# Attention scores ordered behind the mixing products, attention shifted to a later stage, and the state-space scan done in one instruction

## The chip, the cores and the metric

One core of one Trainium2 chip runs the whole layer. The metric is the device time of one execution in microseconds (us). The core has a matrix engine (PE, TensorE), three engines for elementwise work (DVE, which is VectorE; ACT, which is ScalarE; POOL, which is GpSimd) and a queue that issues the DMAs (SP). Each engine works through its own list of instructions in order; semaphores between the lists hold an instruction back until its operands are there.

## The reference

A hybrid block over a sequence of 2048 tokens with 1024 channels, in float32. Two token mixers work side by side on one projection of the normalised input; their outputs are normalised, concatenated and projected back, and a squared-ReLU MLP with 4096 hidden units follows.

```python
xn = rmsnorm(h, norm1_g)
q, k, v, u = split(xn @ w_in)                      # 4 x 512 channels
z = q @ k.T / 8                                    # 8 heads of 64, strictly causal
log_one_minus = where(mask, -softplus(z), 0)
tail = reversed_cumsum(log_one_minus) - log_one_minus
a = where(mask, exp(log_sigmoid(z) + tail), 0)     # stick-breaking weights
sb = a @ v
states = associative_scan(lam_bar, bu)             # 32 groups of 64 complex states
y = gelu(real(states @ c) + d * u)
ssm = y * sigmoid(y @ w_glu + b_glu)
h = h + concat(rmsnorm(sb), rmsnorm(ssm)) @ w_out
out = h + square(relu(rmsnorm(h) @ W1)) @ W2
```

## The kernel before

The sequence is reversed on the host, so that causal sums run forward, and is cut into four quarters of 512 tokens. Matrix operands of the large products are split into a high and a low part, and `mm3` makes each product of three matmuls (high by high, high by low, low by high). Because of that split every product needs an ACT instruction (the high part) and a DVE instruction (the low part) for each operand.

The work is written as Python generators, "streams". `run` takes the next piece from the stream whose virtual time is least; a piece adds its own estimate divided by the stream's weight. So a weight below 1 makes a stream come more seldom. The text order that comes of it is only a priority: a scheduler below it lays out the final list of each engine, with a model of times of its own, and puts an instruction that is ready early ahead of one that is ready late. The lists are then fixed. The stages are:

- `proj_stream` beside `ssm_stream`: 64 jobs of 24 products (1536 matmuls named `m<-w,x`) make q, k, v and u. In the SSM, 16 chains (4 channel blocks, 2 halves of groups, 2 halves of the sequence) each transpose u, multiply by `BT`, rotate by a table (`EC`, `E2`), scan four groups, rotate back into one tile `X`, and multiply by `CP` and `M` (matmuls `m<-CP,X` and `m<-M,uT`); `outputs` then applies GELU. `tables` makes the tables of each block.
- `proj_stream` beside `attn_stream`, in weights 1.0 and 1.0, until the projection is done. A unit of attention is 128 queries of a head against 512 keys; there are 320 units. A unit has two score matmuls (`z`), two ACT sigmoids, a DVE scan (`C`), a POOL multiply, four transposes (`at`), an ACT and a DVE split (`hi`, `lo`) and two matmuls with v (`o`). The transposes and the value products of a unit come seven units behind its scores. A quarter g has 4 - g key blocks for each head, of which one is diagonal and smaller.
- `mix_stream` for the quarter that needs the least (tokens 1536 on) beside attention, weights 1.0 and 1.0. `mix_front` (the gate, 48 products), `mix_body` (the output projection, 192 products) and `mix_tail` (the norm) use products named `m<-h,w 128x512`, 240 in all.
- `plain_up` (1536 products, first MLP layer of two quarters), `mix_stream` for the other quarters in blocks of 256 tokens (`m<-h,w 128x256`, 1440 products), and attention with weight 0.75, until attention has ended.
- `fast_down` for the first half of the output beside the last two blocks of mixing, then `fast_up` and `fast_down` for the other half (products `g`, `fx`, `fy`, `fz`).

Each stage takes its buffers from what the one before it gave back. In the trace the first score starts at 398.6 us, the last projection matmul at 543.5, the first mixing product at 596.3, and the last value product of attention at 1541.4.

Of the kernel before, what the change touches and what calls it, by code (L numbers as in the profile page):

```python
# [62 lines left out]
TWO_PI_INV = 0.6366197723675814  # L63


class Kern:
    def __init__(self, tc, A, out, S):
        self.tc, self.nc, self.A, self.out, self.S = tc, tc.nc, A, out, S
        self.flags = set()
        self.unit = 0  # L70
        self.blocked = {}
# [20 lines left out]
    def mm3(self, ps, lh, ll, rh, rl, start, stop, onto=False):  # L92
        mm = self.nc.tensor.matmul
        mm(ps, lh, rh, start=start, stop=False, skip_group_check=onto)  # L94
        mm(ps, lh, rl, start=False, stop=False, skip_group_check=onto)  # L95
        mm(ps, ll, rh, start=False, stop=stop, skip_group_check=onto)  # L96
# [10 lines left out]
    def consts(self, pool):  # L107
        nc, A = self.nc, self.A
        self.sm = pool.tile([128, NSMALL], F32, name="sm")
        nc.sync.dma_start(out=self.sm, in_=A["small"])  # L110
        self.ident = pool.tile([128, 128], F32, name="ident")
        self.J = pool.tile([128, 128], F32, name="J")
        self.mz = pool.tile([128, 641], F32, name="mz")
        self.ones = pool.tile([128, 128], F32, name="ones")
# [11 lines left out]
    def proj_pools(self, es):  # L126
        tp = lambda n, b: self.pool(es, n, b)
        self.p_xraw = tp("xraw", 2)
        self.p_x = tp("xhl", 4)
        self.p_wraw = tp("wraw", 4)  # L130
        self.p_w = tp("whl", 9)
        self.p_p = tp("pp", 5)
# [128 lines left out]
    def evac(self, Q, gi, j, ps, st, i):  # L261
# [13 lines left out]
        else:  # L275
# [26 lines left out]
            self.pend.append((i + 4, fin))  # L302
# [22 lines left out]
    def attn_stream(self):  # L325
# [30 lines left out]
        def emit_z(b, u):  # L356
            g, h, c = b
            i0 = 128 * u if c == g else 0
            z = self.ps_z.tile([128, 512], F32, tag="z", name="z")
            for m in range(2):  # L360
                nc.tensor.matmul(z[:, i0:512], qt[g, h][m][:, u * 128:(u + 1) * 128], kt[b][:, i0:512],  # L361
                                 start=(m == 0), stop=(m == 1))
            zt[b, u] = z
# [159 lines left out]
    def ssm_params(self):  # L523
# [6 lines left out]
        t = [mk(f"pt{i}") for i in range(6)]  # L530
        ti = mk("pti", W, I32)
        dt = mk("dt")
# [3 lines left out]
        x = mk("px")  # L536
# [5 lines left out]
        sn, cs = mk("sn"), mk("cs")  # L542
        self.sincos(eng, sn, cs, x, t)
        yield 10.0
        lr, li = mk("lr"), mk("li")
# [28 lines left out]
        w1, w2 = mk("pw1", [128, 32, 4]), mk("pw2", [128, 32, 4])  # L574
# [18 lines left out]
        t = [mk(f"pu{i}") for i in range(2)]  # L593
# [26 lines left out]
    def ssm_pools(self, es):  # L620
# [4 lines left out]
        self.m_t = tp("mt", 4)  # L625
        self.m_w = tp("mw", 2)

    def ssm_stream(self):
# [62 lines left out]
        def tables(st, q):  # L691
# [5 lines left out]
            CP = mk("CP", [128, 4, 9, 16])  # L697
            M = Ms[q]
            sl = slice(4 * q, 4 * q + 4)
            gq = slice(8 * st + 4 * q, 8 * st + 4 * q + 4)  # L700
            tabs[st, q] = (EC, E2, BT, CP, M)
# [27 lines left out]
            tt(dve, CP, CP, c1, ALU.add)  # L729
            yield 3.0  # L730
# [12 lines left out]
        def chain(st, q, half):  # L743
# [8 lines left out]
            u2 = self.m_w.tile([128, 4, 8, 16], F32, tag="u2", name="u2", bufs=1)  # L752
# [7 lines left out]
            EC, E2, BT, CP, M = tabs[st, q]  # L760
            X = self.m_w.tile([128, 4, 129], F32, tag="X", name="X", bufs=3)
            Xr = X[:, :, 1:129]
# [13 lines left out]
            for i in range(4):  # L776
                nc.vector.tensor_tensor_scan(
                    out=Xr[:, i, :], data0=prm["rho8"][:, g0 + i:g0 + i + 1].to_broadcast([128, 128]),
                    data1=Xr[:, i, :], initial=0.0 if half else cy[:, i, 3:4], op0=ALU.mult, op1=ALU.add)
            t1, t2 = T([128, 4, 128]), T([128, 4, 128])  # L780
            tt(pool, t1, Xr, EC, ALU.mult)
            nc.scalar.activation(out=t2[0:64], in_=Xr[64:128], func=ACTF.Copy)
            nc.scalar.activation(out=t2[64:128], in_=Xr[0:64], func=ACTF.Copy)
            tt(dve, t2, t2, E2, ALU.mult)
            tt(pool, Xr, t1, t2, ALU.add)
            if half == 1:
                nc.vector.memset(X[:, :, 0:1], 0.0)
                nc.vector.tensor_copy(out=cy[:, :, 0:1], in_=X[:, :, 128:129])
# [5 lines left out]
                tt(dve, cy[:, :, 3:4], cy[:, :, 1:2], cy[:, :, 2:3], ALU.subtract)  # L794
            else:
                nc.vector.tensor_copy(out=X[:, :, 0:1], in_=cy[:, :, 0:1])
# [4 lines left out]
            for i in range(4):  # L801
                o = ps[:, i * 128:(i + 1) * 128]
                nc.tensor.matmul(o, X[:, i, 0:128], CP[:, i, 0:8, :].rearrange("p j h -> p (j h)"),
                                 start=True, stop=False)
                nc.tensor.matmul(o, uT[:, i, :], M[:, i, :], start=False, stop=True)
# [5 lines left out]
        def outputs(st, half):  # L811
            yT = self.m_w.tile([128, 128, 8], F32, tag="c", name="yT", bufs=5)
            for q in range(2):
                ps = self.ps_s.tile([128, 512], F32, tag="m", name="m")
                for i in range(4):
                    nc.tensor.transpose(ps[:, i * 128:(i + 1) * 128], ytm[st, half][:, 4 * q + i, :], self.J)
                a, b = T([128, 512]), T([128, 512])
                nc.scalar.activation(out=a, in_=ps, func=ACTF.Square)
                ts(pool, a, a, 0.044715, ALU.mult, 1.0, ALU.add)
                tt(dve, a, a, ps, ALU.mult)  # L820
                nc.scalar.activation(out=b, in_=a, func=ACTF.Sigmoid, scale=1.5957691216057308)
                tt(dve, yT[:, :, 4 * q:4 * q + 4].rearrange("p c t -> p t c"),
                   b.rearrange("p (t c) -> p t c", t=4), ps.rearrange("p (t c) -> p t c", t=4), ALU.mult)
# [140 lines left out]
    def mix_front(self, X, t0):  # L964
# [12 lines left out]
        for o in range(4):  # L977
            wn = self.load_wt(X, "w_glu", o + 1, 0, 4) if o < 3 else None
            ps = X.ps.tile([128, 512], F32, tag="m", name="m")
            for k in range(4):  # L980
                self.mm3(ps[:, :TB], w[:, 0, k, :], w[:, 1, k, :], yhl[k][:, 0], yhl[k][:, 1], k == 0, k == 3)
                if k % 2:
                    yield mc
# [8 lines left out]
    def mix_body(self, X, b):  # L992
# [6 lines left out]
        for pi, (k0, kk) in enumerate(passes):  # L999
# [5 lines left out]
            for o in range(8):  # L1005
# [9 lines left out]
                for k in range(kk):  # L1015
                    m = b.m[k0 + k]
                    self.mm3(ps[:, :TB], w[:, 0, k, :], w[:, 1, k, :], m[:, 0], m[:, 1], k == 0, k == kk - 1)
# [391 lines left out]
    def run(self, streams, until=None, flag=None):  # L1409
# [3 lines left out]
        while live and flag not in self.flags:  # L1413
# [17 lines left out]
            try:  # L1431
                r = next(gen)
# [9 lines left out]
    def build(self, stop=None):  # L1442
        with ExitStack() as es0:
# [3 lines left out]
            with ExitStack() as el:  # L1447
# [12 lines left out]
                self.run({"proj": (proj, 1.0), "attn": (attn, 1.0)}, until="proj")  # L1460
# [101 lines left out]
```

## Time and profile before

| | |
|---|---|
| median of 3 runs | 2597.24 us (2592.36 to 2602.13) |
| the profiled execution | 2593.43 us, of which the span of the profile is 2591.5 us |
| PE | 2434.2 us busy (94%), 12032 matmuls |
| weight loads (beside PE) | 2009.2 us (78%) |
| DVE | 1943.8 us (75%), 2765 instructions |
| ACT | 1381.3 us (53%), 2628 instructions |
| POOL | 1136.3 us (44%), 1058 instructions |
| HBM | read 395.84 MB, written 134.22 MB |

Matmuls are pipelined: the busy time of one holds its latency, so that a stage can have a nearly full PE row and still issue fewer matmuls in a microsecond than it could. The number of matmuls in a stretch (the x in the tables) is the second thing to read. The product of 128 by 128 by 512 columns is one matmul record; a float32 matmul that isn't of the split kind is recorded as two.

### The profile page before, as it was taken

What the parts mean: (1) busy time and instruction counts of PE and PEld (TensorE: products, weight loads), DVE (VectorE), ACT (ScalarE), POOL (GpSimd) and SP (SyncE); (2) the same over time, 40 slices, a digit from 0 to 9 for tenths busy, and PEclk for the clock granted to TensorE, in tenths of its full rate; (3) what the DMA queues carried; (4) which work ended last, traced back from release to release, by engine and by line L of the source; (5) the groups of instructions that cost most, each with busy time, mean ns of one, the idle gap of its engine ahead of it and who ended that gap; (6) DMA issues with size and microseconds to landing.
All of it is one profiled execution on the core that took longest, in us unless ns stands there. A gap on an engine that the chain in (4) does not pass through costs nothing. (4 is left out here: it accounts for less than half of the span.)

```text
span 2591.5 us, 37361 instructions
## 1 busy us (share of the span) xinstructions
PE 2434.2 (94%) x12032; PEld 2009.2 (78%) x12032; DVE 1943.8 (75%) x2765; ACT 1381.3 (53%) x2628; POOL 1136.3 (44%) x1058
## 2 busy tenths in 40 slices
PE   8898899987888999999999997998999999999999
PEld 6776678865666888888788876886887888887887
DVE  7699978789898787687968863658767666667765
ACT  6454557666465666565656652434444444444443
POOL 5696778678474655464758851140010000003001
PEclk9999999998898999999999998999999999999999
DMA  8635358664563767667786658885674444486565
GB/s 293 201 112 159 118 165 259 174 214 144 175 191 116 252 207 237 223 218 253 254 280 226 216 189 292 298 292 181 207 240 154 142 159 150 145 306 223 180 201 192
DMA packets 352835, 533.74 MB, mean 206 GB/s; under 512 B 34176, under 2 KB 170112, under 8 KB 345344
## 3 DMA queue, kind: packets, MB, share of 16 engines
q1 hardware_dynamic: 352640, 531.36, 62.8%
q8 instruction: 95, 1.56, 0.2%
q14 instruction: 100, 0.82, 0.1%
HBM read 395.84 MB, written 134.22 MB: 205 GB/s over the span
## 5 line engine op out<-in xcount | busy, mean ns | idle before, releaser
L81 POOL TENSOR_TENSOR a<-a,C 128x512 f32<-128x512 f32 (+2 forms) x320 | 437.0, 1372 | 254.9 <-DVE C L385 115.5
L94 PE MATMUL m<-h,w 128*128 128x512 f32 (+1 forms) x1072 | 378.7, 355 | 18.6 <-DMA w<-gluS 9.4
L95 PE MATMUL m<-h,w 128*128 128x512 f32 (+1 forms) x1072 | 376.5, 352 | 5.2 <-DVE h L81 5.2
L96 PE MATMUL m<-h,w 128*128 128x512 f32 (+1 forms) x1072 | 376.4, 352 | 2.5 <-DVE w L81 2.3
L95 PE MATMUL g<-hl 128*128 128x512 f32 x896 | 352.1, 393 | 10.3 <-DVE hl L81 10.3
L96 PE MATMUL g<-hl 128*128 128x512 f32 x896 | 350.8, 392 | 0.0
L385 DVE TENSOR_TENSOR_SCAN C<-s,C,mz 128x513 f32<-128x513 f32 x192 | 305.6, 1600 | 34.9 <-ACT s L376 21.2
L94 PE MATMUL g<-hl 128*128 128x512 f32 x896 | 316.5, 394 | 6.0 <-ACT hl L1138 6.0
L81 POOL TENSOR_TENSOR s<-s,w 128x512 f32<-128x512 f32 x32 | 45.1, 1412 | 486.8 <-DMA ar<-aS 431.7
L1138 ACT ACTIVATE hl<-s 128x512 fp32r<-128x512 f32 x192 | 120.5, 630 | 246.4 <-DVE s L81 92.2
L94 PEld LDWEIGHTS m<-h,w 128*128 128x128 f32 x1072 | 207.3, 194 | 49.6 <-issue 9.9
L95 PEld LDWEIGHTS m<-h,w 128*128 128x128 f32 x1072 | 207.5, 194 | 32.3 <-DVE h L81 6.8
L96 PEld LDWEIGHTS m<-h,w 128*128 128x128 f32 x1072 | 207.1, 193 | 30.0 <-DVE w L81 5.6
L81 DVE TENSOR_TENSOR lo<-at,hi 128x512 fp32r<-128x512 f32 (+1 forms) x320 | 186.4, 593 | 51.6 <-ACT hi L405 51.3
L376 ACT ACTIVATE s<-z 128x512 f32<-128x512 f32 (+1 forms) x320 | 172.9, 541 | 90.1 <-PE z L361 83.4
L405 ACT ACTIVATE hi<-at 128x512 fp32r<-128x512 f32 (+1 forms) x320 | 171.0, 539 | 86.4 <-PE at L401 74.5
L94 PE MATMUL m<-w,x 128*128 128x512 f32 x512 | 207.8, 408 | 8.6 <-ACT w L165 6.0
L95 PE MATMUL m<-w,x 128*128 128x512 f32 x512 | 206.7, 404 | 7.0 <-DVE w L166 7.0
L95 PEld LDWEIGHTS g<-hl 128*128 128x128 f32 x896 | 169.7, 189 | 48.1 <-DVE hl L81 13.4
L96 PE MATMUL m<-w,x 128*128 128x512 f32 x512 | 205.9, 403 | 0.5 <-DVE x L81 0.5
L94 PEld LDWEIGHTS g<-hl 128*128 128x128 f32 x896 | 169.7, 190 | 42.9 <-ACT hl L1138 8.0
L81 DVE TENSOR_TENSOR hl<-s,hl 128x512 fp32r<-128x512 f32 x192 | 137.4, 718 | 83.3 <-ACT hl L1138 78.7
(264 smaller groups left out, 5801.3 us busy)
## 6 DMA issues: line engine op xcount, KB each, us to landing
w<-in_w_dram SPq DMA_DIRECT2D x256, 256.0 KB, 3.6
ar<-aS SPq DMA_DIRECT2D x224, 256.0 KB, 3.4
w<-outS SPq DMA_DIRECT2D x48, 1024.0 KB, 6.4
w<-in_w_dram SPq DMA_DIRECT2D x64, 512.0 KB, 4.2
wr<-in_w_in_dram SPq DMA_DIRECT2D x80, 256.0 KB, 3.8
k<-kS SPq DMA_DIRECT2D x160, 128.0 KB, 3.5
v<-vS SPq DMA_DIRECT2D x80, 256.0 KB, 4.3
aS<-df SPq DMA_DIRECT2D x64, 256.0 KB, 3.0
```

What stands on the lines that cost most here:

```text
L81: eng.tensor_tensor(out=out, in0=a, in1=b, op=op)
L94: mm(ps, lh, rh, start=start, stop=False, skip_group_check=onto)
L95: mm(ps, lh, rl, start=False, stop=False, skip_group_check=onto)
L96: mm(ps, ll, rh, start=False, stop=stop, skip_group_check=onto)
L376: nc.scalar.activation(out=s1[:, 1 + i0:513], in_=z[:, i0:512], func=ACTF.Sigmoid, scale=-0.125)
L385: nc.vector.tensor_tensor_scan(out=C[:, 0:513], data0=s1[:, 0:513], data1=self.mz[:, 128:641], initial=self.C[(n - 4) % 6][:, 512:513], op ...
L405: nc.scalar.activation(out=hi[:, :n], in_=at[:, :n], func=ACTF.Copy)
L1138: nc.scalar.activation(out=t[:, 0], in_=src, func=ACTF.Copy)
```

## The change

Three things are edited together.

The weights of the streams: attention beside the projection goes from 1.0 to 0.55; in the first mixing stage the mixing goes from 1.0 to 2.0; beside the first MLP layer attention goes from 0.75 to 0.95. The `gate`: in the first mixing stage each pair of score matmuls gets an edge that keeps it, in the list of PE alone, behind the last mixing product that was written before it. No semaphore is added.

The SSM chain: the four scans of 128 columns become one scan of 512, whose factor comes from a tile `R` in which the first column of each group is zero; the carried state is added to that column beforehand. The rotation back no longer makes one tile: `Y1` (by `EC`, on POOL) and `Y2` (by `E2`, on DVE) go to PE apart, with a table `CS` that is the swapped and negated `CP`, so each group has three matmuls instead of two. The two DVE multiplies of half height before the scan become two ACT copies and one DVE multiply. GELU drops a POOL instruction, and its transposes now write the tokens interleaved.

Buffers: three weight tiles are read ahead in the projection instead of four (`NW`, `wraw`), `pp` goes from 5 to 4 and the turn of q and k follows three jobs later instead of four; `mt` goes from 4 to 5, and small tables live in shared tiles.

```diff
-        NW = 4
+        NW = 3
...
-            self.pend.append((i + 4, fin))
+            self.pend.append((i + 3, fin))
...
+            with self.tc.issue_after(self.gate) if self.gate else nullcontext():
+                for m in range(2):
+                    nc.tensor.matmul(z[:, i0:512], qt[g, h][m][:, u * 128:(u + 1) * 128], kt[b][:, i0:512],
+                                     start=(m == 0), stop=(m == 1))
...
+            nc.scalar.activation(out=R, in_=prm["rho8"][:, gq].unsqueeze(2).to_broadcast([128, 4, 128]), func=ACTF.Copy)
+            nc.gpsimd.memset(R[:, :, 0:1], 0.0)
...
+            for a, b in ((0, 64), (64, 0)):
+                nc.scalar.activation(out=CS[a:a + 64], in_=CP[b:b + 64, :, 0:8, :].rearrange("p g j h -> p g (j h)"),
+                                     func=ACTF.Copy, scale=-1.0)
...
+            nc.scalar.activation(out=t2[0:64], in_=P[64:128], func=ACTF.Copy)
+            nc.scalar.activation(out=t2[64:128], in_=P[0:64], func=ACTF.Copy)
             tt(dve, t1, P, EC, ALU.mult)
-            tt(dve, t2[0:64], P[64:128], E2[64:128], ALU.mult)
-            tt(dve, t2[64:128], P[0:64], E2[0:64], ALU.mult)
-            tt(pool, Xr, t1, t2, ALU.add)
+            tt(dve, t2, t2, E2, ALU.mult)
+            tt(pool, t1, t1, t2, ALU.subtract)
...
-            for i in range(4):
-                nc.vector.tensor_tensor_scan(
-                    out=Xr[:, i, :], data0=prm["rho8"][:, g0 + i:g0 + i + 1].to_broadcast([128, 128]),
-                    data1=Xr[:, i, :], initial=0.0 if half else cy[:, i, 3:4], op0=ALU.mult, op1=ALU.add)
-            tt(pool, t1, Xr, EC, ALU.mult)
-            nc.scalar.activation(out=t2[0:64], in_=Xr[64:128], func=ACTF.Copy)
-            nc.scalar.activation(out=t2[64:128], in_=Xr[0:64], func=ACTF.Copy)
-            tt(dve, t2, t2, E2, ALU.mult)
-            tt(pool, Xr, t1, t2, ALU.add)
+            nc.vector.tensor_tensor_scan(out=flat(t1), data0=flat(R), data1=flat(t1), initial=0.0,
+                                         op0=ALU.mult, op1=ALU.add)
+            tt(pool, Y1[:, :, 1:129], t1, EC, ALU.mult)
+            tt(dve, Y2[:, :, 1:129], t1, E2, ALU.mult)
...
-                nc.tensor.matmul(o, X[:, i, 0:128], CP[:, i, 0:8, :].rearrange("p j h -> p (j h)"),
+                nc.tensor.matmul(o, Y1[:, i, 0:128], CP[:, i, 0:8, :].rearrange("p j h -> p (j h)"),
                                  start=True, stop=False)
+                nc.tensor.matmul(o, Y2[:, i, 0:128], CS[:, i], start=False, stop=False)
...
-                self.run({"proj": (proj, 1.0), "attn": (attn, 1.0)}, until="proj")
+                self.run({"proj": (proj, 1.0), "attn": (attn, 0.55)}, until="proj")
...
-                self.run({"mix3": (self.mix_stream(X, [1536]), 1.0), "attn": (attn, 1.0)}, until="mix3")
+                self.run({"mix3": (self.mix_stream(X, [1536]), 2.0), "attn": (attn, 1.0)}, until="mix3", gated=True)
...
-                self.run({"attn": (attn, 0.75), "mix": mix, "up": up}, until="attn")
+                self.run({"attn": (attn, 0.95), "mix": mix, "up": up}, until="attn")
```

What this makes of the list of PE, in counts. Before the first score stand 1102 projection products, and with the change 1247. Between the last projection product and the first mixing product stand the scores of 25 units, and now of 7 (units 49 to 74, and 37 to 44). From there to the first product of `plain_up` 63 units, now 53. From that product to its last, 183, now 198; and behind the last product of `plain_up` none are left before, and 25 with the change.

Three places in PE's list. The first is early in the first mixing stage, in the gate's products; `m` is the sum of mixing products (`h` activations, `w` weights), `z` the scores, `at` the transposes, `o` the value products. Before:

```order
L401 MATMUL at<-ident,a 128x128 x2
L420 MATMUL o<-hi,v 128x512
L421 MATMUL o<-lo,v 128x512
L420 MATMUL o<-hi,v 128x384
L361 MATMUL z<-k,qh 128x256
L361 MATMUL z<-k,ql 128x256
L421 MATMUL o<-lo,v 128x384
L401 MATMUL at<-ident,a 128x128
L361 MATMUL z<-k,qh 128x128
L361 MATMUL z<-k,ql 128x128
L94 MATMUL m<-h,w 128x512
L95 MATMUL m<-h,w 128x512
```

With the change, the same stage, from the last two of its first twelve mixing products on:

```order
L97 MATMUL m<-h,w 128x512
L98 MATMUL m<-h,w 128x512
L364 MATMUL z<-k,qh 128x512
L364 MATMUL z<-k,ql 128x512
L96 MATMUL m<-h,w 128x512
L97 MATMUL m<-h,w 128x512
```

Score pairs used to stand wherever they were ready, several units of them between two groups of products; now a pair stands between whole groups of products.

The second place is where `plain_up` ends. Its last three products before (`m_16842`), with transposes and value products around them and no score left:

```order
L420 MATMUL o<-hi,v 128x512
L94 MATMUL m_16842<-h,w_16712 128x512
L95 MATMUL m_16842<-h,w_16712 128x512
L96 MATMUL m_16842<-h,w_16712 128x512
L421 MATMUL o<-lo,v 128x512
L401 MATMUL at<-ident,a 128x128 x4
L420 MATMUL o<-hi,v 128x512
```

And with the change (`m_16614`), where attention goes on without other work for 25 pairs of scores:

```order
L97 MATMUL m_16614<-h,w_16495 128x512
L98 MATMUL m_16614<-h,w_16495 128x512
L364 MATMUL z<-k,qh 128x512
L364 MATMUL z<-k,ql 128x512
L423 MATMUL o<-hi,v 128x512
L424 MATMUL o<-lo,v 128x512
L404 MATMUL at<-ident,a 128x128 x4
L423 MATMUL o<-hi,v 128x512
```

The third is behind attention's last value product, where `fast_down` (products `g`) and the last mixing blocks begin. Before, 36 products `g` come first, and then the norm and 48 mixing products in one piece; their seam:

```order
L95 MATMUL g<-hl 128x512
L96 MATMUL g<-hl 128x512
L891 MATMUL m<-ones,acc 128x1 x2
L897 MATMUL m<-ident,rc 128x128 x2
L94 MATMUL m<-h,w 128x256
L95 MATMUL m<-h,w 128x256
```

With the change 12 mixing products come first, then groups of 18 `g` and 12 mixing products in turn; the first seam:

```order
L96 MATMUL m<-h,w 128x256
L97 MATMUL m<-h,w 128x256
L98 MATMUL m<-h,w 128x256
L96 MATMUL g<-hl 128x512 x3
L97 MATMUL g<-hl 128x512
```

The mixing products, whose weights come by DMA one group at a time, now have products `g` between their groups.

More of the change, by code (lines that the diff above doesn't have):

```diff
@@ L1 @@
-from contextlib import ExitStack
+from contextlib import ExitStack, nullcontext
 import numpy as np
@@ L70, in __init__ @@
         self.unit = 0
+        self.gate = self.last = None
         self.blocked = {}
@@ L113, in consts @@
         self.mz = pool.tile([128, 641], F32, name="mz")
-        self.ones = pool.tile([128, 128], F32, name="ones")
+        self.ones = pool.tile([128, 1], F32, name="ones")
         nc.vector.memset(self.ones, 1.0)
@@ L529, in ssm_params @@
         mk = lambda n, w=W, dt=F32: pool.tile(w, dt, name=n)
-        t = [mk(f"pt{i}") for i in range(6)]
-        ti = mk("pti", W, I32)
-        dt = mk("dt")
+        scr = self.m_t.tile([128, 18, 32], F32, tag="tt", name="scr", bufs=3)
+        t = [scr[:, i] for i in range(6)]
+        ti = scr[:, 6].bitcast(I32)
+        dt, x, sn, cs, lr, li = (scr[:, i] for i in range(7, 13))
         self.exp_poly(eng, dt, self.small("ldt"), t, ti)
@@ L573, in ssm_params @@
         nc.vector.tensor_copy(out=PI[:, :, 1:2], in_=li.unsqueeze(2))
-        w1, w2 = mk("pw1", [128, 32, 4]), mk("pw2", [128, 32, 4])
+        pw = self.m_t.tile([128, 2, 32, 4], F32, tag="tt", name="pw", bufs=3)
+        w1, w2 = pw[:, 0], pw[:, 1]
         n = 1
@@ L592, in ssm_params @@
         eng = nc.gpsimd
-        t = [mk(f"pu{i}") for i in range(2)]
+        t = [scr[:, i] for i in range(13, 15)]
         pc, pp = mk("phc", [128, 32, 11]), mk("phs", [128, 32, 11])
@@ L759, in chain @@
             yield 1.0
[L760 to L762 removed]
+            EC, E2, BT, CP, CS, R, M = tabs[st, q]
             ps = self.ps_s.tile([128, 512], F32, tag="m", name="m")
@@ L775, in chain @@
             cy = carry[st, q]
[L776 to L785 removed]
+            if not half:
+                tt(dve, t1[:, :, 0:1], t1[:, :, 0:1], cy[:, :, 3:4], ALU.add)
+            nc.vector.tensor_tensor_scan(out=flat(t1), data0=flat(R), data1=flat(t1), initial=0.0,
+                                         op0=ALU.mult, op1=ALU.add)
+            Y1 = self.m_w.tile([128, 4, 129], F32, tag="Y1", name="Y1")
+            Y2 = self.m_w.tile([128, 4, 129], F32, tag="Y2", name="Y2")
+            tt(pool, Y1[:, :, 1:129], t1, EC, ALU.mult)
+            tt(dve, Y2[:, :, 1:129], t1, E2, ALU.mult)
+            nc.gpsimd.memset(Y2[:, :, 0:1], 0.0)
             if half == 1:
[L787 to L788 removed]
+                nc.gpsimd.memset(Y1[:, :, 0:1], 0.0)
+                nc.vector.tensor_copy(out=cy[0:64, :, 1:2], in_=Y2[64:128, :, 128:129])
+                nc.vector.tensor_copy(out=cy[64:128, :, 1:2], in_=Y2[0:64, :, 128:129])
+                tt(dve, cy[:, :, 0:1], Y1[:, :, 128:129], cy[:, :, 1:2], ALU.subtract)
                 se = cy[:, :, 0:1]
@@ L1406, in fast_down, with run @@
             yield 2.7
-    def run(self, streams, until=None, flag=None):
+    def run(self, streams, until=None, flag=None, gated=False):
         vt = {n: 0.0 for n in streams}
@@ L1431, in run @@
             try:
+                if gated:
+                    self.gate = self.last
                 r = next(gen)
@@ L1465, in build @@
                 X = self.mix_pools(el, 512, "left", ps3, p_hn)
-                self.run({"mix3": (self.mix_stream(X, [1536]), 1.0), "attn": (attn, 1.0)}, until="mix3")
+                self.run({"mix3": (self.mix_stream(X, [1536]), 2.0), "attn": (attn, 1.0)}, until="mix3", gated=True)
+            self.gate = self.last
             ep.close()
```

40 lines of the change are left out of this document (19 added, 21 removed).

## The prediction

> **What bounds the kernel now.** I read the busy times first, then the stretches between the events where the kernel changes stage, then who waited for whom in the worst stretch.
>
> ```profile
> PE 2434.2 (94%) x12032; PEld 2009.2 (78%) x12032; DVE 1943.8 (75%) x2765; ACT 1381.3 (53%) x2628; POOL 1136.3 (44%) x1058
> ...
> core 0: us, PE busy (x) PEld busy (x) DVE busy (x) ACT busy (x) POOL busy (x), PEclk, DMA share, GB/s
> 0.00:398.00 398.00, 351.41 (x1780) 286.85 (x1781) 332.13 (x630) 210.23 (x351) 286.13 (x350) 0.96 0.57 178
> 398.00:596.00 198.00, 185.26 (x960) 153.05 (x959) 162.32 (x211) 139.24 (x299) 155.33 (x158) 0.97 0.71 210
> 596.00:802.00 206.00, 162.17 (x723) 125.14 (x722) 187.20 (x210) 121.55 (x259) 136.88 (x111) 0.85 0.51 157
> 802.00:1541.00 739.00, 727.58 (x4025) 614.76 (x4024) 580.70 (x643) 459.77 (x914) 463.83 (x361) 0.99 0.69 226
> 1541.00:1600.00 59.00, 39.99 (x193) 34.33 (x194) 20.78 (x43) 20.26 (x43) 7.05 (x9) 0.77 0.81 292
> ```
>
> PE is the bound of the whole: 94% busy. It isn't the bound everywhere. From 802 to 1541 (the first MLP layer with attention) it idles for 739 - 728 = 11 us and runs at full clock. From 596 to 802 (the first mixing stage) it idles for 44 us of 206, its granted clock (PEclk) is 0.85, and it issues 723/206 = 3.5 matmuls in a microsecond against 5.4 in the next stage; there DVE is busy for 187 of 206 us. So that stage goes at DVE's pace. The first stretch, with the SSM, idles PE for 47 of 398 us with DVE at 83%. The short stretch from 1541 idles it for 19 of 59.
>
> ```profile
> PE o L421 <- DVE lo L81: 13.2, 6, 4.0
> PE m L95 <- DVE h L81: 4.9, 2, 3.4
> ```
>
> These are the two longest waits of PE from 596 to 755: engine and line that waited, what released it, us in total, times, longest. Both are for splits on DVE, attention's first.
>
> **Prices.** DVE, from 543 to 802, by group (count, busy us, mean ns):
>
> ```profile
> L385 DVE TENSOR_TENSOR_SCAN C<-s,C,mz 128x513 f32<-128x513 f32 x48 | 77.4, 1626 | 3.5 <-ACT s L376 3.3
> L81 DVE TENSOR_TENSOR lo<-at,hi 128x512 fp32r<-128x512 f32 (+1 forms) x84 | 47.7, 577 | 10.3 <-ACT hi L405 10.2
> L379 DVE TENSOR_TENSOR_SCAN C<-s,mz 128x384 f32<-128x384 f32 (+3 forms) x39 | 39.0, 1018 | 2.3 <-issue 1.5 <-ACT s L376 0.6
> L81 DVE TENSOR_TENSOR sb<-o,tmp 64x512 f32<-64x512 f32 x10 | 6.7, 665 | 0.0
> ```
>
> They make (77.4 + 47.7 + 39.0 + 6.7) / 87 scans = 1.96 us of DVE for a unit of attention. PE's price is read from where it never waits, by the starts of what follows each other:
>
> ```profile
> 1500.31 0.40 PE L95 MATMUL m<-h,w 128*128 128x512 f32 x1
> 1500.55 0.40 PE L361 MATMUL z<-k,qh 128*128 128x512 f32 x1
> 1500.78 0.40 PE L361 MATMUL z<-k,ql 128*128 128x512 f32 x1
> 1501.01 0.39 PE L96 MATMUL m<-h,w 128*128 128x512 f32 x1
> ...
> 1514.88 0.60 PE L401 MATMUL at<-ident,a 128*128 128x128 f32 x4
> 1515.23 0.48 PE L420 MATMUL o<-hi,v 128*128 128x512 f32 x1
> 1515.55 0.39 PE L421 MATMUL o<-lo,v 128*128 128x512 f32 x1
> 1515.78 0.60 PE L401 MATMUL at<-ident,a 128*128 128x128 f32 x4
> ```
>
> A product or a score takes 0.23 us, four transposes 0.35, the value pair 0.32 + 0.23: 1.36 us for a full unit, and I take 1.2 with the smaller diagonal ones in. So a unit costs DVE more than PE: alone it leaves PE idle, beside products it doesn't.
>
> **The change, stage by stage.** I sum against the profiled execution, 2593.43 us (its span is 2591.5), which is 3.8 us below the median of the runs.
>
> *To the first score (398 us before).* In PE's list 145 more projection products now stand ahead of it: 145 x 0.23 = 33 us, work that is only moved. New are the products with `CS`:
>
> ```profile
> 371.79 0.49 PE L803 MATMUL m<-CP,X 128*128 128x128 f32 x2 [0.72 <-POOL X L81]
> 372.11 0.39 PE L805 MATMUL m<-M,uT 128*128 128x128 f32 x2
> 372.34 0.39 PE L803 MATMUL m<-CP,X 128*128 128x128 f32 x2
> ```
>
> A pair of records takes 372.34 - 372.11 = 0.23 us; 64 pairs make 14.5 us, the one thing that PE really gets more of. On DVE:
>
> ```profile
> L777 DVE TENSOR_TENSOR_SCAN X<-rho,X 128x128 f32<-128x128 f32 x32 | 22.1, 748 | 5.2 <-POOL X L81 5.2
> L777 DVE TENSOR_TENSOR_SCAN X<-rho,carry,X 128x128 f32<-128x128 f32 x32 | 16.2, 567 | 0.3
> L81 DVE TENSOR_TENSOR t<-m,E 64x512 f32<-64x512 f32 x32 | 22.0, 688 | 0.5
> L81 DVE TENSOR_TENSOR t<-t,E 128x512 f32<-128x512 f32 x16 | 13.1, 816 | 5.8 <-ACT t L783 5.4
> L81 DVE TENSOR_TENSOR carry<-carry 128x4 f32<-128x4 f32 x8 | 1.3, 159 | 0.0
> ...
> L385 DVE TENSOR_TENSOR_SCAN C<-s,C,mz x192: 1252/1289/2404, 500.7 to 1514.8; 128x513 f32<-128x513 f32 x192
> ```
>
> The four scans cost (22.1 + 16.2)/16 = 2.4 us a chain. One scan of 512 columns is not in the trace; its nearest row is attention's scan of 513 (last line: minimum, median, maximum), 1.25 to 2.40 us, and I take the mean of the first price row, 1.6: 16 x 0.8 = 13 us gained, between 0 and 18. The half-height multiplies (22.0 us) give way to one more of the `t<-t,E` kind (13.1): 9 us gained. Some 32 more small instructions on the carried state, at the 0.16 us of the row `carry<-carry`, add 5 us. GELU's interleaved transposes and last multiply have no row of their kind; I take no gain and no loss, between -7 and +7 us. So DVE loses some 17 us of work, and POOL a sum and a GELU step a chain:
>
> ```profile
> L81 POOL TENSOR_TENSOR X<-t 128x512 f32<-128x512 f32 x32 | 49.9, 1568 | 20.4 <-DVE t L81 20.4
> L78 POOL TENSOR_SCALAR t<-t 128x512 f32<-128x512 f32 x16 | 11.2, 701 | 9.2 <-ACT t L818 8.2
> ```
>
> 16 x (1.57 + 0.70) = 36 us. The ACT copies of `CS` and `R` and the weight tile less that is read ahead I cost at nothing: ACT is busy for 210 of 398 us, and PE has the projection's other products to go on with; without that cover the 24 copies cost 24 x 0.60 = 14 us, at 210.23/351 = 0.60 us for an ACT instruction of this stretch. DVE and PE then take turns less often, and I let PE's idle time of 47 us fall to 20. The first score comes at 398 + 33 + 14 - 27 = 418.
>
> *To the first mixing product (198 us before).* The 145 products are gone from here (-33), and 30 units of attention (74 before, 44 now, the cheap early ones: 1.1 us each, -33), and idle time goes from 13 to 5. That makes 124 us: 542 instead of 596. The 25 units that stood alone between the last projection product and the first mixing product are now 7, so this gap closes, and what takes its place as the last to be ready is the split of y on DVE.
>
> *The first mixing stage (206 us before).* DVE sets it; 10 units fewer take 19.6 us from its 187. At the same share the stage takes 185 us, and ends at 727 instead of 802. The gate adds no wait by itself: it sets the order in PE's list, and behind a score held back stand only that unit's sigmoids and scan.
>
> *The first MLP layer (739 us before).* The 15 units more beside the products go at PE's price: 18 us. The 25 left over stand alone. Their price is that of the 25 units that stood alone before:
>
> ```profile
> 543.00:596.00 53.00, 40.29 (x206) 30.80 (x206) 45.61 (x56) 39.00 (x86) 40.12 (x39) 0.90 0.76 241
> ```
>
> 53 us, or 2.1 each, so again DVE's pace. With 7 us of draining and 9 us that the old end and the moved lag give back, the stage takes 739 + 18 + 53 + 7 - 9 = 808 and ends at 1535 instead of 1541. The 75 us won up to there are nearly all paid back here.
>
> *The start of the second layer (59 us before).*
>
> ```profile
> PE m L94 <- DMA w<-gluS: 7.2, 1, 7.2
> PE g L94 <- ACT hl L1138: 3.1, 1, 3.1
> ```
>
> PE's longest wait is for a weight of the mixing by DMA, with 48 mixing products in one piece. Groups of `g` now stand between, 18 products of 0.23 us or 4 us each; I take 14 us off. Later stages do the same work.
>
> Sum: -6 - 14 = -20 on 2593.43, 0.8%; on the median 2597.24 - 20 = **2577 us**.
>
> **The rivals.** (1) *The tail is cheaper and the SSM stage dense.* For it speaks that PE idles for only 13 us in the second stretch, where DVE is at 82%. If the idle time before the first score falls to 10 and the tail loses half of its 23 us (53 us less 25 x 1.2 of work): 10 + 11 less, 2556.
>
> (2) *The SSM edit nets nothing.* `Y1` on POOL and `Y2` on DVE start together after the scan, and read the same tile.
>
> ```profile
> 551.05 1.11 DVE L81 TENSOR_TENSOR w<-wr,w 128x512 fp32r<-128x512 f32 x1
> 553.76 0.71 DVE L81 TENSOR_TENSOR w<-wr,w 128x512 fp32r<-128x512 f32 x1
> ```
>
> The same DVE instruction takes 0.71 or 1.11 us, so something holds it up. If each `Y2` waits out a POOL instruction like the sum above, 1.57 us, DVE gets 16 x 1.57 = 25 us back, more than the 17 saved, and the idle time stays at 47: 2577 + 27 = 2604, no change. The Trainium skill ("SBUF — State Buffer", section Who interferes with whom) states just this: a DVE instruction with two SBUF inputs contends with a GpSimd instruction that reads SBUF, and the one that comes second is blocked. The spread of that row agrees; which of the two comes second here no run shows. Against it: POOL has 36 us less to do, so it meets DVE less often.
>
> (3) *Slower: the gate starves attention.* If the splits that the mixing products need come late on the device, the scores stand behind a group of 12 products that can't start, and DVE, which sets the stage, runs empty. There are 20 such groups; if each costs DVE the 1.7 us of an ACT and a DVE split (0.60 and 1.11), the stage grows by 34 us, and by twice that where attention's seven units of lead must fill again: the middle is 2577 + 50 = 2627. It decides when DVE's busy share in the mixing stage drops from 91% to under 75%. Against it: in the rows above PE waits for the mixing's `h` for only 4.9 us. That the change doesn't move what it says is no case: the list of PE shows the scores moved.
>
> **How the numbers follow.** Forecast: 0.50, with its own range of 2560 to 2597, the bounds of the scan, GELU and the tail. Rival 1: 0.20. Rival 2: 0.17. Rival 3: 0.13. A measurement of this kernel can tell 0.5% from no change, 13 us, so faster means below 2584 and slower above 2610. About two thirds of the forecast (0.34) and all of rival 1 lie below: 0.54 faster. Rival 3 is slower: 0.13. The rest, 0.33, is no change. The range from 2545 to 2612 leaves out most of rival 3 and a little below rival 1.
>
> **What would show it.** Right: the first score near 418 us with PE idle for 20 before it; the first mixing product near 542; the first MLP product near 727; some 25 units alone at 2.1 us; the last value product near 1535; less than 10 us idle after it. Wrong: a `Y2` multiply much over 0.8 us (rival 2), DVE under 75% in the mixing stage (rival 3), or a lone tail under 45 us (rival 1).

## The result, and the profile after

The changed kernel takes 2583.95 us (median of 14 runs, 2571.51 to 2588.55) where the kernel before takes 2597.43 us in the same runs. The ratio is 0.9941, with a 95% interval of 0.9926 to 0.9955: 13.5 us less in the medians, 15 by the ratio; 2577 was predicted. Its profiled execution has a span of 2579.1 us against 2591.5. The parts of the sum come out less well than the sum.

The busy row of the page, and the stretches of the changed kernel between the events that the prediction used (length; busy us and number of instructions of PE, PEld, DVE, ACT and POOL; granted clock, DMA share, GB/s):

```profile
PE 2430.1 (94%) x12160; PEld 2013.2 (78%) x12160; DVE 1932.3 (75%) x2725; ACT 1393.8 (54%) x2652; POOL 1135.0 (44%) x1058
...
0.00:432.00 432.00, 396.83 (x2080) 328.36 (x2081) 332.60 (x615) 243.24 (x402) 271.85 (x362) 0.98 0.59 181
432.00:547.00 115.00, 107.56 (x562) 90.59 (x561) 89.32 (x122) 78.98 (x177) 95.48 (x101) 0.97 0.72 209
547.00:726.00 179.00, 142.65 (x654) 110.06 (x654) 154.41 (x193) 108.83 (x230) 118.15 (x97) 0.89 0.63 193
726.00:1480.00 754.00, 737.30 (x4071) 623.94 (x4072) 607.15 (x661) 468.67 (x951) 498.15 (x389) 0.99 0.71 226
1480.00:1549.00 69.00, 51.61 (x249) 37.03 (x247) 62.03 (x63) 44.20 (x88) 50.98 (x31) 0.93 0.25 73
1549.00:1608.00 59.00, 53.33 (x257) 43.96 (x257) 29.89 (x55) 26.71 (x57) 8.48 (x9) 0.91 0.87 324
```

The boundaries are the first score (432), the first mixing product (547), the first and last product of the first MLP layer (726, 1480), and attention's last value product (1549). The kernel is 49 us ahead at 547 and 77 ahead at 726, and at 1549 it is 7 us behind. Attention alone, from 1480, has DVE busy for 62.0 of 69 us and PE for 51.6. The first 59 us of the second layer hold 257 matmuls, 193 before.

The instructions that the state-space edit brought to DVE, from 100 to 432 us (count, busy us, mean ns, idle before):

```profile
L785 DVE TENSOR_TENSOR_SCAN t<-R,t 128x512 f32<-128x512 f32 x16 | 22.3, 1395 | 1.7 <-POOL t L83 1.4
...
L83 DVE TENSOR_TENSOR t<-t,E 128x512 f32<-128x512 f32 x16 | 13.9, 871 | 0.0
L83 DVE TENSOR_TENSOR Y<-t,E 128x512 f32<-128x512 f32 x16 | 12.8, 800 | 0.1
...
L83 DVE TENSOR_TENSOR yT<-t,m 128x512 f32<-128x512 f32 x16 | 10.9, 684 | 7.0 <-ACT t L831 7.0
...
L795 DVE COPY carry<-Y 64x4 f32<-64x4 f32 x8 | 8.9, 1109 | 0.1
```

The scan of 512 columns takes 1.40 us where four took 2.4: 16 us saved, 13 forecast. Of the small copies of the carried state, one group is much dearer than forecast (1.1 us in the mean where 0.16 was taken).

Three stretches need a cause that the change's own description doesn't give: why the gap before the first mixing product closed, what the state-space edit is worth, and why the late stages, whose work is the same, got shorter. The first product of `fast_up` starts at 1955.5 before and 1949.9 after, so 7 us (2591.5 - 1955.5 = 636.0 against 2579.1 - 1949.9 = 629.2) come from there.

### The profile page after: what moved, and what is told of

Its sections match the earlier page's. It is cut to its first block, busy times and chain, and to the rows that moved or that the text cites. A ratio compares the mean times of both kernels' runs of the same rounds, so it can differ in the third digit from the quotient of the medians.

```text
span 2579.1 us, 37634 instructions
## 1 busy us (share of the span) xinstructions
PE 2430.1 (94%) x12160; PEld 2013.2 (78%) x12160; DVE 1932.3 (75%) x2725; ACT 1393.8 (54%) x2652; POOL 1135.0 (44%) x1058
## 5 line engine op out<-in xcount | busy, mean ns | idle before, releaser
L83 POOL TENSOR_TENSOR a<-a,C 128x512 f32<-128x512 f32 (+1 forms) x320 | 460.6, 1447 | 232.3 <-DVE C L388 106.3
L388 DVE TENSOR_TENSOR_SCAN C<-s,C,mz 128x513 f32<-128x513 f32 x192 | 318.3, 1663 | 28.4 <-ACT s L379 17.3
```

Of the source, the lines that this page charges most:

```text
L83: eng.tensor_tensor(out=out, in0=a, in1=b, op=op)
L388: nc.vector.tensor_tensor_scan(out=C[:, 0:513], data0=s1[:, 0:513], data1=self.mz[:, 128:641], initial=self.C[(n - 4) % 6][:, 512:513], op ...
```

## The experiments

Each was run beside the kernel before, on the same chip; a ratio is to those runs. "Loss" is worked out from all starts of matmuls: what the next start comes later than the median for a product of that kind, summed over a stretch. The time of an event is that of one profiled execution: in five kernels (the changed one, and those with the old weights, without the gate, with the weight 2.4 and with `h` moved) the same 1247 projection products stand ahead of the first score, and it comes at 431.9 to 435.7 us. So differences of a few us between such times say little.

### The tile of ones alone

```diff
-        self.ones = pool.tile([128, 128], F32, name="ones")
+        self.ones = pool.tile([128, 1], F32, name="ones")
```

> The kernel before with one edit of the change's SSM part: the tile of ones is 128x1 instead of 128x128 and so takes 508 bytes less of each SBUF partition; the tiles allocated behind it on that side, `ty` of fast_up among them, start at 32 instead of 0 modulo 64 bytes. The order of TensorE's instructions is that of before. Theory A (start address): the products of fast_up, 512 columns each, go from 0.2335 to 0.227 us from start to start as they did in the changed kernel, 1344 x 6.5 ns = 8.7 us, so 2588.7 where before is 2597.4; first score, first mixing product and attention's end stay where before has them. Theory B (the changed order, or less work beside them, makes the late stages faster): fast_up's products stay at 0.2335 us and the time at 2597.

Measured: 2594.37 us, ratio 0.9973 (0.9960 to 0.9987). Two groups of products of `fast_up`, by line, in the kernel before:

```profile
L94 PE MATMUL fy<-ty,hl 128*128 128x512 f32 x192 | 76.0, 397 | 0.0
L95 PE MATMUL fy<-ty,hl 128*128 128x512 f32 x192 | 75.9, 396 | 0.0
```

and of this kernel:

```profile
L94 PE MATMUL fy<-ty,hl 128*128 128x512 f32 x192 | 74.9, 391 | 0.0
L95 PE MATMUL fy<-ty,hl 128*128 128x512 f32 x192 | 74.8, 390 | 0.3 <-DVE ty L81 0.3
```

From start to start they take 0.227 us, 0.234 before; without the loss, the work from `fast_up` on is 609.1 us where it was 617.6 (609.1 in the changed kernel). With the whole order unchanged, moving the tiles by 480 bytes gives the pace; of the two operands of these products only `ty` is among them, the weight tile `hl` stays where it was. Theory A holds, and some 7 us (0.27%) of the result are this.

### State-space edit without the streams; streams without it; no gate

The first has the old weights and no gate, the second only weights and gate on the kernel before, the third the changed kernel with

```diff
-                self.run({"mix3": (self.mix_stream(X, [1536]), 2.0), "attn": (attn, 1.0)}, until="mix3", gated=True)
-            self.gate = self.last
+                self.run({"mix3": (self.mix_stream(X, [1536]), 2.0), "attn": (attn, 1.0)}, until="mix3")
```

> The changed kernel with the old weights of the streams (1.0, 1.0, 0.75) and no gate: the SSM edit, its buffers and the small tile of ones alone. Theory A (the streams only move time; address and SSM edit carry the gain): 2597.4 - 8.7 by the address, and what the SSM edit is worth by itself, DVE's 17 us of work less 14.5 us of new CS products less the read-ahead that is one tile shorter, 0 +- 6: 2583 to 2594. Theory B (the gain is the streams' alone): no less than 2597, with DVE's saving given back as PE idle time for the weight read-ahead. The prediction's own steps, without the address, would have -2 to +3 here: 2595 to 2600.

> The kernel before with the stream weights (0.55, 2.0, 0.95) and the gate alone: SSM, buffers and the tile of ones as before, so fast_up's products at 0.2335 us. Theory A (streams pay back inside the attention stages): attention ends within 10 us of 1541, the start of the second layer (from there to the first product of fast_up) is 12 us shorter as in the changed kernel, so 2583 to 2597, most likely 2588. Theory B (all of the gain is address and SSM edit): 2597 or more. If the read-ahead of four weight tiles keeps PE's idle time before the first score at 47 us or less with 33 us of moved products, the first score comes near 425.

> The changed kernel without the gate (weights, SSM edit and buffers as changed). Theory A (the gate only sets an order that the scheduler would have within a few places; DVE sets the stage): within 5 us of the changed kernel's 2584, DVE's share in the first mixing stage stays near 86%. Theory B (without it the scores get ahead of the mixing products and hold them up behind a full PSUM): the first mixing stage grows by 10 us or more, 2594 and above. Theory C (the gate starves attention as the third rival had it): the stage gets shorter, DVE's share rises over 90%, and 2570 to 2578.

Measured: state-space edit with its buffers and ones 2585.86 us, 0.9940 (0.9926 to 0.9955), the changed kernel's own ratio and within theory A (the next runs show that its gain is the buffers', not the edit's). Streams alone 2608.52 us, 1.0032 (1.0021 to 1.0043): theory B, and slower than the kernel before; its first score, for which near 425 was expected, comes at 401.3. Without the gate 2586.62 us, 0.9944 (0.9927 to 0.9962): the gate does nothing that can be measured, theory A; DVE is busy for 163.5 of the 185 us of that mixing stage.

The lists of these runs also say which edit moves what. Projection products ahead of the first score: 1102 before, 1102 with the streams alone, 1131 with the smaller buffers, 1247 as soon as the state-space edit is added to these, with the old weights as with the new. Units ahead of the first mixing product: 74 before, 54 with the streams alone or the buffers alone, 44 with the state-space edit. So the weight 0.55 moves no product ahead of the first score. What the prediction counted there as the change's 145 moved products comes from the state-space edit (116) and the buffers (29).

The streams' run shows what holds the first mixing product. These are waits of ACT and PE in it, from 540 to 605 us (engine and line that waited, what released it, us in total, times, longest):

```profile
ACT hi L297 <- DMA kS<-hi: 5.8, 2, 3.4
...
ACT h L907 <- DMA kS<-lo: 3.4, 1, 3.4
...
PE m L95 <- ACT h L907: 10.3, 1, 10.3
```

PE waits 10.3 us for `h`, the split of y; ACT, which makes it, waits for the store of `lo`, the last turned key tile of the projection. No data goes from one to the other. By the program's allocation they share memory: the first split of y lies at 120512 to 124607 of a partition, and `lo` (2048 bytes) at 121536.

### The buffers

The first of three runs is the kernel before with the smaller buffers alone; the others are its halves, `pp` with the earlier turn, and the weight tiles with their read-ahead.

```diff
-        self.p_wraw = tp("wraw", 4)
+        self.p_wraw = tp("wraw", 3)
...
-        self.p_p = tp("pp", 5)
+        self.p_p = tp("pp", 4)
...
-        NW = 4
+        NW = 3
...
-            self.pend.append((i + 4, fin))
+            self.pend.append((i + 3, fin))
```

> The kernel before with the smaller buffers of the change alone: three tiles of weights read ahead instead of four, four `p` tiles instead of five, the projection's ends due one product earlier; the state-space scan and the stream weights as before. Theory A (the read-ahead costs): TensorE waits longer for weights before the first score, 20 us more as ScalarE's wait for them rose from 15.5 to 32.5 us in the changed kernel, so 2605 to 2620. Theory B (other products cover it, the longer wait of the changed kernel comes from its faster state-space stage): 2594 to 2602, and the loss before the first score stays near 53 us.

> Half of the smaller buffers: four `p` tiles instead of five and the projection's ends due one product earlier; weights still read four tiles ahead. By its instruction order the first mixing product stands after 71 units of attention, where before has 74 and both halves together 54. Theory A (the gain is the closed gap ahead of the first mixing product, for which it takes both halves): little of it, 0.998 to 1.001, and TensorE still loses some 25 us between first score and first mixing product. Theory B (the earlier ends alone keep the projection's stream free): 0.994 to 0.996.

> The other half: three tiles of weights read ahead instead of four; the projection's ends as before. By its instruction order the first mixing product stands after 71 units of attention, where before has 74 and both halves together 54. Theory A (the gain takes both halves): 0.998 to 1.002, with the gap ahead of the first mixing product still open. Theory B (the shorter read-ahead alone lets the state-space stage have ScalarE and DVE earlier): 0.994 to 0.996. Theory C (the read-ahead is missed): 1.002 or more.

Measured: both halves 2584.70 us, 0.9935 (0.9914 to 0.9956); the earlier turn 2596.61 us, 0.9975 (0.9965 to 0.9985); the shorter read-ahead 2595.48 us, 0.9979 (0.9966 to 0.9992). So the buffers alone give as much as the whole change, which no theory had: both of the first run's expected no gain, and theory A of the halves (it takes both) is nearest, though each half gives a little more than it allowed. In the traces, with addresses of the allocation:

| | `lo` at | shared with the first split of y | last key store issued | first split of y | first mixing product |
|---|---|---|---|---|---|
| before | 121536 | 2048 bytes | 590.6 us | 593.6 us | 596.3 us |
| earlier turn | 119488 | 1024 | 589.0 | 595.1 | 596.2 |
| shorter read-ahead | 119488 | 1024 | 593.8 | 600.0 | 601.7 |
| both | 117440 | none | 582.3 | 563.4 | 564.1 |
| changed kernel | 116960 | none | 565.7 | 539.5 | 546.8 |

Wherever a byte is shared, y is split after the last store; where none is, it is split 19 to 26 us ahead of it. The rows of the kernel before, its timeline from 587 to 597 us (start, duration, engine, line):

```profile
588.30 0.69 ACT L296 ACTIVATE hi<-m,sm 128x512 fp32r<-128x512 f32 x1
589.01 0.36 SPq L300 DMA_DIRECT2D kS<-hi  x1
589.81 0.73 DVE L297 SCALAR_TENSOR_TENSOR lo<-m,sm,hi 128x512 fp32r<-128x512 f32 x1
590.57 0.36 SPq L300 DMA_DIRECT2D kS<-lo  x1
...
593.63 2.31 ACT L905 ACTIVATE h<-y 128x512 fp32r<-128x512 f32 x4
```

The store of `lo` lands at 592.8 by its semaphore, and the split starts 0.8 us later. y itself was asked for at 543.9 and landed at 548.9. The programs show the dependency too: where bytes are shared, the split's instruction waits for the semaphore of this last store (before, either half by itself, streams alone); in the kernel with both halves and in the changed one it waits for a single semaphore, that of y's own load. The list of PE is laid out with this dependency in it: between the last projection product and the first mixing product stand 25 units of attention before, 22 and 23 with the halves, and 6 with both. That is the gap that the prediction saw. In the run with both halves the loss from first score to first mixing product is 10.6 us, before 27.6, and in the mixing stage 64.5, before 78.9.

### Buffers and ones, without and with the streams

The two parts found, neither state-space edit nor streams; and the same with the weights and the gate.

> The kernel before with the change's smaller buffers (as in the run with the buffers alone, 0.9935) and its small tile of ones (0.9973 alone), and neither the state-space edit nor the streams. Theory A (the two add, since one acts in the first two stretches and the other in fast_up): 0.9935 x 0.9973 = 0.9908, about 2575 where before is 2599; fast_up's products at 0.227 us; then the state-space edit and the streams of the changed kernel (0.9941) together cost some 8 us. Theory B (the two don't add): 0.9935 to 0.9945, 2582 to 2586, and the state-space edit is worth nothing either way.

> As the run before it, with the stream weights and the gate as changed: all of the change but the state-space edit. Theory A (the streams' price is the lone tail, some 25 us of lost TensorE time against 13 us won at the start of the second layer, with or without the smaller buffers): 5 to 12 us slower than the run without them, 2580 to 2588; attention ends near 1548. Theory B (the streams cost only where the gap ahead of the first mixing product is open, as in the kernel before): within 3 us of the run without them. What the changed kernel takes less than this one is what the state-space edit is worth beside them.

Measured: 2574.23 us, 0.9893 (0.9875 to 0.9911), the fastest of all, below the changed kernel; theory A, whose 0.9908 lies in the interval. With the streams 2587.43 us, 0.9949 (0.9929 to 0.9969): nearest to theory A, 13 us slower where it said 5 to 12, and attention ends at 1557.8 where it said 1548. The stretches of the kernel with buffers and ones alone:

```profile
0.00:406.00 406.00, 359.46 (x1819) 288.70 (x1820) 326.15 (x635) 214.05 (x357) 286.24 (x355) 0.97 0.58 178
406.00:556.00 150.00, 145.63 (x764) 121.68 (x762) 120.15 (x161) 103.69 (x225) 121.92 (x123) 1.00 0.73 203
556.00:743.00 187.00, 151.66 (x683) 116.87 (x682) 167.78 (x205) 118.09 (x247) 141.24 (x102) 0.87 0.65 195
743.00:1517.00 774.00, 758.70 (x4195) 641.93 (x4195) 622.02 (x687) 489.92 (x987) 505.31 (x400) 0.99 0.69 221
1517.00:1525.00 8.00, 6.27 (x29) 3.66 (x27) 4.38 (x7) 4.00 (x7) 1.27 (x1) 1.00 0.65 198
```

With the four kernels that have buffers and ones, both other parts are seen with and without each other (us in the profiled execution; units of attention by the list of PE):

| | ratio | first score | first mixing product | units by then | last MLP product | units left | attention's end | first of `fast_up` |
|---|---|---|---|---|---|---|---|---|
| neither | 0.9893 | 406.0 | 555.9 | 54 | 1516.7 | 0 | 1524.6 | 1937.7 |
| state-space edit | 0.9940 | 435.7 | 555.1 | 44 | 1516.7 | 5 | 1542.6 | 1956.5 |
| streams | 0.9949 | 411.5 | 560.4 | 54 | 1490.9 | 25 | 1557.8 | 1955.6 |
| both (the change) | 0.9941 | 431.9 | 546.8 | 44 | 1480.3 | 25 | 1548.7 | 1949.9 |

The state-space edit costs 0.0047 (12 us) without the streams and nothing that can be measured beside them (0.9949 to 0.9941). The first two rows agree at the first mixing product and at the last MLP product, but with the edit ten units fewer are done by the first mixing product and five are left at the end, alone. ("State-space edit" has in it all that is left of the change: `mt`, the shared small tables and the GELU edit were not tried apart.) The streams cost 13 us without the edit, and nothing beside it: 20 to 25 units more stand alone, and the start of the second layer is 12 to 15 us shorter.

### Without the products of CS; attention earlier; h moved by 32 bytes

```diff
-                nc.tensor.matmul(o, Y2[:, i, 0:128], CS[:, i], start=False, stop=False)
```

> The changed kernel without the products of CS and Y2, one of the four terms summed into the state-space output (64 products, 128 records); the sine part of the state's contribution is left out. Theory A (TensorE sets the first stretch, as the step of the prediction that adds 14.5 us has it): 14 us shorter before the first score, 2570. Theory B (DVE and the weights set it, the products are hidden): the first score stays within 4 us of 432, and 2580 to 2584.

Measured: 2588.52 us, 0.9959 (0.9944 to 0.9973), no gain on 0.9941, and above the 2580 to 2584 of theory B as well. The first stretch to its first score:

```profile
0.00:431.00 431.00, 393.86 (x1964) 320.68 (x1965) 327.27 (x616) 243.74 (x403) 274.11 (x362) 0.96 0.59 180
```

As theory B has it, the first score stays within 4 us of 432. But more than these products changed. The list was laid out anew and has 1260 projection products ahead of the first score instead of 1247 (3 us), and the granted clock was 0.96, in the changed kernel 0.98. Of the 11 us of TensorE work that are gone on balance, at most 5 come through, against the five kernels with 1247; the rest is loss again, here some 70 us to the first score and 59 in the changed kernel. So taking these products out buys next to nothing; what holds TensorE in their place isn't shown. In its list 43 units are done by the first mixing product, not 54, so these products are not what took the ten units either.

```diff
-                self.run({"attn": (attn, 0.95), "mix": mix, "up": up}, until="attn")
+                self.run({"attn": (attn, 2.4), "mix": mix, "up": up}, until="attn")
```

> The changed kernel with a weight of 2.4 instead of 0.95 for attention beside the first MLP layer, so that by the instruction order no unit of attention is left over behind the last MLP product. In the changed kernel TensorE loses 28.7 us in the 68.5 us of the lone tail, and 36 us at the start of the second layer where before lost 49. Theory A (the tail is DVE's pace with nothing beside it; beside the MLP there is room): the tail's 29 us of loss go, the start of the second layer is 13 us dearer again as in the kernel before, since it can fetch nothing ahead during the tail: 2584 - 16 = 2568. Theory B (the tail only collects what DVE lacks, 80% busy beside the MLP already): the MLP stage loses as much more, 2578 to 2590.

Measured: 2633.40 us, 1.0126 (1.0103 to 1.0149), a miss of both theories. The lone tail does go, from 68.5 to 11.5 us, and although the MLP stage takes 794 us instead of 754, both together take 805 instead of 823: theory A's gain is there. But the start of the second layer breaks: these are its first 123 us,

```profile
1537.00:1660.00 123.00, 75.52 (x386) 65.56 (x387) 31.12 (x76) 28.80 (x67) 18.94 (x24) 0.73 0.64 222
```

and those of the changed kernel:

```profile
1549.00:1672.00 123.00, 117.33 (x608) 99.85 (x608) 68.30 (x118) 50.16 (x103) 17.70 (x20) 0.96 0.90 324
```

In its list the mixing stands in pieces of 48 and 192 products with only the norms between and no product `g`, so that every wait of a norm or a weight is a wait of PE:

```profile
PE m L96 <- DVE h L83: 9.6, 5, 7.5
PE m L900 <- POOL acc L83: 9.1, 3, 4.2
PE m L906 <- POOL rc L83: 7.0, 5, 2.7
PE m L96 <- DMA w<-gluS: 6.6, 2, 5.8
```

What the interleaving with `g` is worth is seen here from the other side: from attention's end to `fast_up` this kernel takes 466 us, the changed one 401, before 414.

```diff
+            self.pool(eh, "hpad", 1, None, "right").tile([128, 8], F32, name="hpad")
             p_hn = self.pool(eh, "hn", 8, None, "right")
```

> The changed kernel with 32 bytes per partition left unused ahead of the buffer of `h`, so that `h` starts at 32 instead of 0 modulo 64 bytes, with the instruction order unchanged. Theory A (the moving tile's start address sets the pace of a dense 512-column product): the 1536 products of the first MLP layer and the 240 of the first mixing stage go from 0.234 to 0.227 us from start to start, up to 1776 x 6.5 ns = 11.5 us, less where DVE sets the pace: 2573 to 2580. Theory B (fast_up's pace came from something else): 0.234 us stays, and 2584.

Measured: 2585.64 us, 0.9954 (0.9941 to 0.9967): no gain, theory B. The products of the first MLP layer go from 0.234 to 0.232 us from start to start and not to 0.227. So the start address modulo 64 alone isn't the rule; that the place of `ty` mattered is shown, why isn't.

## Why the prediction was right, and where not

**The sum.** Forecast -20 us, measured -12.4 between the two profiled spans and -15 by the ratio. That the time lay in the range is in part luck, because terms that were missing on both sides nearly cancel: buffers and ones give 28 us (1 - 0.9893), and state-space edit and streams together take 12 back (0.9941 - 0.9893).

**First score: 418 forecast, 432 measured.** The step that failed is "I let PE's idle time of 47 us fall to 20": PE idles for 432 - 397 = 35 us. PE's own work rose as forecast, from 351.4 to 396.8 us (45, where 33 + 14.5 was taken). But the 17 us of DVE's work that were to make the stretch denser were not saved: DVE is busy for 1921.9 us of the whole kernel with buffers and ones, and for 1921.0 with the state-space edit added. The scan did get cheaper; some of that went to the small copies. By the last `yT` the state-space work ends later, although this multiply itself is cheaper. The kernel with buffers and ones:

```profile
L81 DVE TENSOR_TENSOR yT<-t,m x16: 1069/1152/1200, 202.6 to 401.5; 128x512 f32<-128x512 f32 x16
```

and the changed kernel (minimum, median and maximum in ns, first and last start):

```profile
L83 DVE TENSOR_TENSOR yT<-t,m x16: 673/686/690, 210.7 to 426.2; 128x512 f32<-128x512 f32 x16
```

The last chain's products with `CP` stand behind 1184 projection products in the changed list and behind 1045 in the other. The first score comes 30 us later with the edit (435.7 against 406.0), and that nearly adds up: 116 more projection products ahead of it are 26 us of work that is only moved, the `CS` products 14.5, and some 12 us less is lost. Why the list came out so was not tried.

**First mixing product: 542 forecast, 547 measured.** The count of units gave the right size for the stretch (115 us measured, 124 forecast), but what closes the gap was missed. The prediction read the closed gap off the list and gave the buffers no part in it: of them it names only "the weight tile less that is read ahead", at nothing. The smaller buffers are the largest gain of the change, 17 us by themselves (0.9935), and they end the sharing of memory between `lo` and `h`. The streams alone leave 33 us between the last projection product and the first mixing product, and the buffers alone 12.

**First mixing stage: 185 us forecast, 179 measured.** The mechanism, fewer units at DVE's pace, holds: DVE is busy for 86% of it.

**The lone tail: 53 + 7 us forecast, 69 measured.** The mechanism, DVE's pace, holds; the size is off by 9 us. The price of 2.1 us a unit was the length of the stretch from 543 to 596 before, whose 25 units are early ones: 11 of its 22 scans have the longest form, and DVE is busy for 45.6/25 = 1.8 us a unit.

```profile
L385 DVE TENSOR_TENSOR_SCAN C<-s,C,mz 128x513 f32<-128x513 f32 x11 | 17.8, 1642 | 0.0
```

In the tail of the changed kernel 22 of 26 scans have it, and DVE is busy for 62.0/25 = 2.5 us a unit:

```profile
L388 DVE TENSOR_TENSOR_SCAN C<-s,C,mz 128x513 f32<-128x513 f32 x22 | 39.0, 1783 | 0.9 <-issue 0.9
```

This is most of why attention ended at 1549 instead of 1535: the MLP layer itself began at 726, as forecast.

**Start of the second layer: -14 forecast.** To the first product of `fast_up` it is 414.1 - 401.1 = 13 us shorter. Every kernel with the new weights up to 0.95 has it (398 to 402 us) and has products `g` between 12 mixing products in its list; every one with the old weights hasn't (412 to 417) and has 36 `g` and then 48 mixing products. Right, cause and size.

**"Later stages do the same work."** They do, but 7 us faster, by the smaller tile of ones.

**The rivals.** The first needed a cheaper tail, and it was dearer. The second said that the state-space edit nets nothing, and that is what was measured, but not for its reason: `Y2` takes 677 ns at least, 682 in the median and 800 in the mean, so the 16 of them wait for 16 x (800 - 682) = 1.9 us and not for 25; the saving is missing all the same, as said above. The Trainium skill ("SBUF — State Buffer", section Who interferes with whom) has the second of two such instructions blocked; the longest here, 1766 ns, may be such a one, but the median shows that most are not held up. The third fell: DVE's share stayed at 86%, and the gate can be left out.

Left open: why the list with the state-space edit puts more projection products ahead of attention, what the edit's 12 us without the streams are made of, and whether only the shared bytes make the buffers' gain (moving `h` away with the old buffers was not tried; the halves' own 0.2% have no cause shown).

## What to carry to other kernels

When a change shrinks or moves a buffer, compare the allocation before and after: a tile that reuses the memory of another waits for its last reader, and a static list of instructions is built around that wait. Before a stage's instructions are made cheaper, take some of them out as a trial; if the stage keeps its length, but for a few us, as here without the `CS` products, making them cheaper will not help. Compare the lists of the two kernels as well, since the scheduler puts other work in the place. And measure the parts of a change apart: here four numbers of the buffers and one small tile beat the whole.

## What the runs showed that was not expected

- A dense 512-column product of `fast_up` goes from 0.234 to 0.227 us from start to start when its moving tile `ty` starts at 32 instead of 0 modulo 64 bytes; the same move of `h` gives 0.234 to 0.232 us in the first MLP layer.
- The mixing's interleaving with the next layer's products is worth as much as 466 - 401 = 65 us, and a stream weight that concerns neither of them decides it.
